# Gate and up by seven half-size products, then the down product by quarters

## The chip, the cores and the metric

One core of a Trainium2 chip runs the kernel. The metric is device time in microseconds (us), the median of three executions. A fourth execution was profiled; all rows below are from it.

## The reference

Two transformer-like blocks over 512 tokens of width 2048, float32, one after the other. Only the last part of the second block changes:

```python
h = rmsnorm_2(x, g_pre_ffn) * (1.0 + sc_f) + sh_f
f = (jax.nn.silu(h @ w_gate) * (h @ w_up)) @ w_down      # 2048 -> 5632 -> 2048
x = x + gt_f * rmsnorm_2(f, g_post_ffn)
```

## The kernel before

Every large product is done in float32 accuracy from three passes: each operand is split into a rounded high part (`fp32r`) and the low rest, and hi·hi, hi·lo and lo·hi are summed in PSUM. The weights stream through a list of *pieces* made in `make_plan`: a piece is 256 rows (two k tiles of 128) by 512 columns. SyncE (SP) loads it as `raw` (four buffers), ScalarE (ACT) rounds it to `whi`, VectorE (DVE) subtracts to get `wlo` (three buffers each); `piece()` keeps the split three pieces ahead of TensorE (PE).

`gemm` consumes pieces: for each k tile and each of four PSUM tiles (banks) it issues the three matmuls. With `half` it does 256 tokens instead of 512. TensorE's order is the order of the program. The other engines are ordered by the tile framework, and each runs its own list strictly in turn. Small work that is to run beside the matmuls (`side`) is issued a step per k tile (`tick`).

The feed-forward part works on `F`, 16 tiles of the transposed activations (they appear as `M` in rows), 128 features by 512 tokens, each in two parts. A *column group* is 256 columns of gate and the same 256 of up, so 22 groups make the 5632 columns. Groups 0 and 1 are done in two token halves, behind the end of the attention output (`w_out2`); the others are one `gemm` of 512 tokens. `up` takes the four PSUM tiles of a group, multiplies silu(gate) by up, and splits the result `u` into two parts that stay in SBUF. After every two groups `down` multiplies those four `u` tiles (stationary, 128 tokens each) by 512 rows of `w_down` and adds the result to `f`. The last `down` is ordered by token blocks, so that the norm, the scaling and the store of one block lie beside the matmuls of the next. PSUM has eight banks: five in the pool `mm`, three in `aux`.

Of the kernel before, what the change touches and what calls it, by code (L numbers as in the profile page):

```python
# [39 lines left out]
class Kernel:  # L40
    def __init__(self, ctx, tc, a, out):
        self.tc, self.nc, self.a, self.out = tc, tc.nc, a, out
        pool = lambda name, **kw: ctx.enter_context(tc.tile_pool(name=name, **kw))
        self.cp = pool("cp", bufs=1)
        self.wp = pool("wp", bufs=1)
        self.t4p = pool("t4p", bufs=30)
        self.t2p = pool("t2p", bufs=8)
        self.bigp = pool("bigp", bufs=1)
# [4 lines left out]
        self.sides = []  # L53
        self.make_plan()


    def make_plan(self):
# [3 lines left out]
        add = lambda segs, k0=0, nk=KT: groups.append((segs, k0, nk))  # L61
# [37 lines left out]
        self.pieces = [(segs, k0 + k) for segs, k0, nk in groups for k in range(0, nk, self.KP)]  # L99
# [3 lines left out]
    FFN = [("u", 0), ("u", 1)] * 2  # L103
    for _n in range(11):
        FFN += [("u", 2 * _n + 2), ("d", _n), ("u", 2 * _n + 3)] if _n < 10 else [("d", _n)]
# [49 lines left out]

    def mm(self):
        return self.mmp.tile([P, S], F32, tag="mm", name=self.name("mm"))
# [4 lines left out]
    def row(self, s):  # L162
        return self.cp.tile([P, S], F32, tag="row", name=self.name(s))
# [25 lines left out]
    def prefetch(self, nload, nsplit):  # L189
        nc, KP = self.nc, self.KP  # L190
        while self.loaded < min(nload, len(self.pieces)):
            segs, k0 = self.pieces[self.loaded]
            raw = self.wp.tile([P, KP, S], F32, tag="raw", bufs=4, name=self.name("raw"))
            o = 0
# [5 lines left out]
            self.raw[self.loaded] = raw  # L200
            self.loaded += 1
        while self.halved < min(nsplit, len(self.pieces)):
            raw = self.raw.pop(self.halved)
            if self.halved < len(self.pieces) - 8:
                hi = self.wp.tile([P, KP, S], F32R, tag="whi", bufs=3, name=self.name("whi"))
                lo = self.wp.tile([P, KP, S], F32R, tag="wlo", bufs=3, name=self.name("wlo"))
            else:
                hi, lo = self.pair("whi"), self.pair("wlo")
            for k in self.parts(self.halved):
                h, l, r = hi[:, k], lo[:, k], raw[:, k]  # L210
                if self.halved < 2 * KT // KP:
# [5 lines left out]
            self.wts[self.halved] = (hi, lo)  # L217
            self.halved += 1
# [131 lines left out]
    def scale_x(self, k):  # L350

        raw, g = self.xt[k], self.cols["norm_gain"][:, k:k + 1]
        pr = self.X[k] = self.pair("X")
        self.act(pr[:, 0, :], raw, AF.Identity, scale=g)
        self.stt(pr[:, 1, :], raw, g, pr[:, 0, :].bitcast(F32), MUL, SUB)
        if k == 0:
            self.ssx = self.const("rxrow", [P, S])
        self.sumsq(self.ssx, raw, k == 0)
# [11 lines left out]
    def ssm_scalars(self):  # L370
# [18 lines left out]
        pr, pi = c("acc1", [P, 9, G]), c("acc2", [P, 9, G])  # L389
# [361 lines left out]
    def ple(self):  # L751
# [6 lines left out]
        acc = [self.const("acc1", [P, S]), self.const("acc2", [P, S])]  # L758
        self.rrow, self.rxrow = self.row("rrow"), self.const("rxrow", [P, S])
# [92 lines left out]
    def ada_steps(self):  # L852
# [4 lines left out]
        def load(i):  # L857
            if i < 192 and i not in st:
                c, kp = divmod(i, 8)
                st[i] = self.t4("wa", [P, 2, S])  # L860
                nc.sync.dma_start(st[i], w[kp * 256:(kp + 1) * 256, c * S:(c + 1) * S].rearrange("(a p) n -> p a n", p=P))

        def step(c, kp):
            load(c * 8 + kp)
            load(c * 8 + kp + 1)
# [299 lines left out]
    def w_out2(self):  # L1165

        nc, a = self.nc, self.a
        mo = []
        acc = [self.const("acc1", [P, S]), self.const("acc2", [P, S])]
        prow, frow = self.row("rrow"), self.const("rxrow", [P, S])  # L1170
# [56 lines left out]
        us = {}  # L1227
        for n in range(2):
            us[n] = self.up(self.gemm(F, half=0), slice(0, 256))
        self.finish(s)  # L1230
        for n in range(2):
            self.up(self.gemm(F, half=1), slice(256, S), us[n])
        self.F, self.M = F, None
# [10 lines left out]
        self.side([lambda b=b, q=q: turn(b, q) for q in range(4) for b in range(4)], 16)  # L1244
        return us

    def up(self, ps, cs=slice(0, S), us=None):

        us = us or [self.pair("u") for _ in range(2)]
        for i in range(2):  # L1250
            t = self.t2("u")
            self.act(t[:, cs], ps[i][:, cs], AF.Silu)
            self.tt(t[:, cs], t[:, cs], ps[2 + i][:, cs], MUL)
            self.nc.scalar.copy(us[i][:, 0, cs], t[:, cs])
            self.tt(us[i][:, 1, cs], t[:, cs], us[i][:, 0, cs].bitcast(F32), SUB)
        return us

    def ffn(self, us):
        nc = self.nc
        f, r, x2 = [], [None] * 4, {}  # L1260
        fv = lambda b, q: f[b * 2 + q // 2][:, q % 2, :]
        out = self.out.rearrange("o s d -> (o s) d")

        def down(n, us):
            if n == 0:
                f.extend(self.t4("f", [P, 2, S]) for _ in range(8))
            for q in range(4):
                ps = self.gemm(us, tok=True)
                for b in range(4):
                    if n == 0:  # L1270
                        nc.vector.tensor_copy(fv(b, q), ps[b])
                    else:
                        self.tt(fv(b, q), fv(b, q), ps[b], ADD)

        def gain():
            co = self.const("cogf", [P, 16])
            self.tt(co, self.mod[:, 80:96], self.cols["g_post_ffn_2"], MUL)
            self.G = self.bigp.tile([P, 4, S], F32, tag="big", name="G")
            for q in range(4):
                self.rows(self.G[:, q, :], co[:, 4 * q:4 * q + 4], 4)  # L1280
                yield

        def x2_load(b, q):
            x2[b, q] = self.t2("x2")
            nc.sync.dma_start(x2[b, q], self.x2d[b * P:(b + 1) * P, q * S:(q + 1) * S])

        ada = self.side([None] * 20 + self.ada(20, 24), 200)
        for kind, n in self.FFN[4:-1]:
            if kind == "u":
                us[n] = self.up(self.gemm(self.F))  # L1290
            else:
                down(n, us.pop(2 * n) + us.pop(2 * n + 1))
            if n == 12 and kind == "u":
                self.finish(ada)
                self.side(self.steps(gain(), 5), 10)
        self.F = None
        us = us.pop(20) + us.pop(21)
        w = [[self.piece() for _ in range(2)] for _ in range(4)]
        ss = self.const("ssf", [P, 4, 4])
        for b in range(4):  # L1300
            for q in range(4):
                x2_load(b, q)
                ps = self.mm()
                for k in range(4):
                    hi, lo = w[q][k // 2]
                    for j, (xi, wt) in enumerate(((0, hi), (1, hi), (0, lo))):
                        nc.tensor.matmul(ps, us[k][:, xi, b * P:(b + 1) * P], wt[:, k % 2, :],  # L1307
                                         start=(k == 0 and j == 0), stop=(k == 3 and j == 2))
                self.tt(fv(b, q), fv(b, q), ps, ADD)
                junk = self.t4("fq", [P, S])  # L1310
                self.act(junk, fv(b, q), AF.Square, accum_out=ss[:, b, q:q + 1])
                self.tt(fv(b, q), fv(b, q), self.G[:, q, :], MUL)
# [3 lines left out]
            for q in range(4):  # L1316
                self.stt(x2[b, q], fv(b, q), r, x2[b, q], MUL, ADD)
                nc.sync.dma_start(out[b * P:(b + 1) * P, q * S:(q + 1) * S], x2[b, q])
# [57 lines left out]
def blocks(K, a, dbg):  # L1376
# [52 lines left out]
    K.ffn(K.w_out2())  # L1429
# [15 lines left out]
```

## Time and profile before

| | us |
|---|---|
| median of 3 executions (3309.81 to 3311.39) | 3310.8 |
| profiled execution, device time | 3309.45 |
| its span, first to last instruction | 3307.4 |
| TensorE busy | 3223.1 (97%) |
| VectorE busy | 1951.2 (59%) |
| ScalarE busy | 1143.7 (35%) |

The device time has 2.05 us more than the span, for what lies around it. Busy time of TensorE counts overlapping matmuls once; a matmul's own record is longer than the step from one matmul to the next, so the step is read from start times.

### The profile page before, as it was taken

The numbers are of one execution on the slowest core, as the hardware profiler recorded it, in microseconds if no ns is written. First come the engines' busy times: TensorE is split into PE (matmuls) and PEld (weight loads), VectorE is DVE, ScalarE is ACT, GpSimd is POOL, SyncE is SP. The second block draws the span as 40 slices with busy tenths as digits, with TensorE's granted clock in tenths as the row PEclk, the third lists the DMA queues.
The fourth block names the chain that finished last, engine by engine and source line by source line (L and its number), as shares of the span: only waits on it lengthen the run. The fifth ranks groups of instructions, "written<-read, shape, count | busy, mean of one in ns | idle before, by whom it ended". The sixth has DMA issues, their size and how long they took to land.

```text
span 3307.4 us, 42034 instructions
## 1 busy us (share of the span) xinstructions
PE 3223.1 (97%) x16076; PEld 2699.6 (82%) x16076; DVE 1951.2 (59%) x3736; ACT 1143.7 (35%) x1679; POOL 15.5 (0%) x28
## 2 busy tenths in 40 slices
PE   7998999999999999999998899999999999999998
PEld 6886887788899777787788888888888888888886
DVE  8569557867798576867748837523333233233336
ACT  6332443223456363434435531222222222222222
POOL 0000000000000000000000000000000000000000
PEclk9999999999999999999999999999999999999999
DMA  6554544756558443434335557433333333333334
GB/s 194 180 194 161 169 156 156 260 168 205 185 172 268 134 141 126 161 128 153 102 106 179 178 173 244 140 97 101 96 96 96 96 96 98 99 96 96 96 98 144
DMA packets 333130, 482.51 MB, mean 146 GB/s; under 512 B 29456, under 2 KB 173968, under 8 KB 332928
## 3 DMA queue, kind: packets, MB, share of 16 engines
q1 hardware_dynamic: 326912, 466.28, 44.3%
q0 software_dynamic: 1664, 5.57, 0.7%
q10 hardware_dynamic: 4352, 7.96, 0.7%
q8 instruction: 126, 2.06, 0.3%
q14 instruction: 76, 0.62, 0.1%
HBM read 454.64 MB, written 25.10 MB: 145 GB/s over the span
## 4 chain that ended last, share of the span: by engine, by line
PE 85%; DVE 10%; DMA 2%; ACT 2%; issue 1%; SPq 0%; DVEq 0%; ACTq 0%
PE mm L245 61%; PE mm L243 18%; DVE wlo L170 2%; PE probs L1009 2%; PE mix L1057 1%; DMA wa<-in_w_ada_dram 1%; DVE sc L170 1%; DVE ada L179 1%; PE turn L1049 1%; ACT whi L215 1%; DVE acc L170 1%; PE mm L595 1%; PE mm L1307 0%; PE mm L596 0%; PE kk L504 0%
## 5 line engine op out<-in xcount | busy, mean ns | idle before, releaser
L170 DVE TENSOR_TENSOR wlo<-raw,whi 128x1024 fp32r<-128x1024 f32 (+1 forms) x607 | 752.9, 1242 | 956.9 <-ACT whi L215 944.5
L215 ACT CAST whi<-raw 128x1024 fp32r<-128x1024 f32 (+1 forms) x607 | 651.1, 1074 | 1591.1 <-PE mm L245 1052.0
L245 PE MATMUL mm<-M,whi 128*128 128x512 f32 (+1 forms) x3840 | 1060.8, 363 | 2.6 <-ACT qk L979 1.3
L245 PEld LDWEIGHTS mm<-M,whi 128*128 128x128 f32 x3840 | 689.8, 190 | 112.4 <-ACT qk L979 1.7
L245 PE MATMUL mm<-M,wlo 128*128 128x512 f32 (+1 forms) x1920 | 695.7, 362 | 5.7 <-DVE wlo L170 5.7
L245 PE MATMUL mm<-H,whi 128*128 128x512 f32 (+1 forms) x2048 | 513.2, 343 | 2.3 <-ACT pp L805 2.3
L245 PEld LDWEIGHTS mm<-M,wlo 128*128 128x128 f32 x1920 | 364.4, 190 | 61.7 <-DVE wlo L170 6.5
L243 PE MATMUL mm<-whi,u 128*128 128x512 f32 x1280 | 395.2, 390 | 1.0 <-ACT u L182 0.8
L245 PEld LDWEIGHTS mm<-H,whi 128*128 128x128 f32 x2048 | 347.1, 191 | 49.2 <-issue 9.8
L245 PE MATMUL mm<-H,wlo 128*128 128x512 f32 (+1 forms) x1024 | 345.9, 338 | 1.5 <-DVE wlo L170 1.5
L245 PE MATMUL mm<-X,whi 128*128 128x512 f32 x1024 | 325.3, 399 | 7.6 <-ACT whi L215 7.2
L179 DVE SCALAR_TENSOR_TENSOR ada<-wa,siluc,ada 128x512 f32<-128x512 f32 x360 | 269.8, 749 | 50.5 <-DMA wa<-in_w_ada_dram 45.3
L243 PEld LDWEIGHTS mm<-whi,u 128*128 128x128 f32 x1280 | 239.7, 188 | 51.6 <-ACT u L182 1.2
L243 PE MATMUL mm<-wlo,u 128*128 128x512 f32 x640 | 249.3, 389 | 0.0
L245 PEld LDWEIGHTS mm<-X,whi 128*128 128x128 f32 x1024 | 190.5, 191 | 48.3 <-ACT whi L215 7.2
L245 PEld LDWEIGHTS mm<-H,wlo 128*128 128x128 f32 x1024 | 194.7, 190 | 22.9 <-DVE wlo L170 1.7
L245 PE MATMUL mm<-X,wlo 128*128 128x512 f32 x512 | 201.6, 394 | 1.2 <-DVE wlo L170 1.2
L243 PE MATMUL mm<-whi,H 128*128 128x512 f32 x512 | 162.7, 399 | 0.0
L243 PEld LDWEIGHTS mm<-wlo,u 128*128 128x128 f32 x640 | 120.2, 188 | 25.0
L170 DVE TENSOR_TENSOR f<-f,mm 128x512 f32<-128x512 f32 x160 | 109.1, 688 | 47.2 <-PE mm L243 45.8
L245 PEld LDWEIGHTS mm<-X,wlo 128*128 128x128 f32 x512 | 97.0, 190 | 23.3 <-DVE wlo L170 2.2
L243 PEld LDWEIGHTS mm<-whi,H 128*128 128x128 f32 x512 | 93.7, 188 | 21.3 <-issue 3.1
(323 smaller groups left out, 2930.6 us busy)
## 6 DMA issues: line engine op xcount, KB each, us to landing
wa<-in_w_ada_dram SPq DMA_DIRECT2D x192, 512.0 KB, 5.9
raw<-in_w_in_dram SPq DMA_DIRECT2D x111, 512.0 KB, 3.7
raw<-in_w_gate_dram SPq DMA_DIRECT2D x192, 256.0 KB, 2.8
raw<-in_w_up_dram SPq DMA_DIRECT2D x192, 256.0 KB, 3.1
raw<-in_w_down_dram SPq DMA_DIRECT2D x88, 512.0 KB, 3.8
raw<-in_w_out_dram SPq DMA_DIRECT2D x80, 512.0 KB, 4.4
raw<-in_w_in_dram SPq DMA_DIRECT2D x130, 256.0 KB, 3.0
raw<-in_w_ple_gate_dram SPq DMA_DIRECT2D x48, 512.0 KB, 4.6
```

The lines of the kernel that those rows point to most:

```text
L170: self.nc.vector.tensor_tensor(o, x, y, op=op)
L179: self.nc.vector.scalar_tensor_tensor(o, x, s, y, op0=op0, op1=op1)
L215: nc.scalar.copy(h, r)
L243: nc.tensor.matmul(ps[i], x[k][:, xi, c], wt[:, a, :], **fl)
L245: nc.tensor.matmul(ps[i][:, cs], wt[:, a, c], x[k][:, xi, cs], **fl)
L595: nc.tensor.matmul(out, self.U[j][:, h, g, :], T[:, :, g, :], start=True, stop=False)
L1009: nc.tensor.matmul(ps[:, :n], q[:, i * P:n], k[:, :n], start=True, stop=True)
L1049: nc.tensor.transpose(pt[:, b * P:(b + 1) * P], p[:, b * P:(b + 1) * P], self.ident)
L1057: nc.tensor.matmul(po[:, :P], pT[:, b * P:(b + 1) * P], v(b, h), start=(b == 0), stop=(b == i))
```

## The change

- The plan no longer alternates. Gate and up come first for all 22 groups: groups 0 and 1 in token halves and group 2 whole, as before; groups 3 to 21 by `seven`. The down product follows, by quarters.
- `seven` (Strassen's scheme in the variant with few additions): the 2048 rows are halved (k tiles k and k+8), the tokens are halved (256 each), and the 256 columns of gate, and those of up, are halved into tiles of 128, so that a group is a product of 2x2 blocks. Seven block products replace eight. Each product runs over 8 pieces k, and in each over gate and up (`s`), with three matmuls of 256 tokens. Seven PSUM banks hold the seven products until the group ends.
- The activations' sums are made once (`sums`, eight calls, during groups 0 to 2). The weights' sums are made for each piece (`halve_sums`): four float32 additions of 128x256 on VectorE, one of them in place in `raw`, and two splits, of the four weight blocks (128x1024: `whi`, `wlo`) and of three sums `T` (128x768: `thi`, `tlo`).
- At the end of a group the four blocks of the result are put together from the seven banks (`ev`: one ScalarE copy `c`, seven VectorE operations), then silu and product (`fin`), and `u` goes to DRAM (`us`) by GpSimd's queue. What comes after product 3 is handed to the next group (`rest`, `todo`), a step after each product. In this stage ScalarE and VectorE run in the order of the program.
- A piece of this stage is loaded by six DMAs instead of two.
- Down by quarters: 512 output columns at a time over all 44 row tiles, summed in PSUM, so that `f` is written once. `u` is read back from DRAM and split again for each quarter (the six pieces at a quarter's turn stay). The last four pieces of the last quarter are ordered by token blocks.

```diff
-        for kind, n in self.FFN:
-            if kind == "u":
-                add([(g2, n * 256, 256), (u2, n * 256, 256)])
-            else:
-                for q in range(4):
-                    add([(d2, q * S, S)], 4 * n, 4)
+        for n in (0, 1, 0, 1, *range(2, self.NS)):
+            add([(g2, n * 256, 256), (u2, n * 256, 256)])
+        for n in range(self.NS, self.NU):
+            groups.append((((g2, n * 256), (u2, n * 256)), range(-8, 0)))
+        for q in range(4):
+            groups.append(([(d2, q * S, S)], self.down_order(q)))
...
+    NU, NS, STAY = DFF // 256, 3, 6
...
+        def one():
+            self.tt(t[:, :, 0], b(0), b(1), ADD)
+            self.tt(b(1), b(1), b(2), ADD)
+            nc.scalar.copy(hv, v)
+
+        def two():
+            self.tt(t[:, :, 1], t[:, :, 0], b(2), ADD)
+            self.tt(t[:, :, 2], t[:, :, 1], b(3), ADD)
+            nc.scalar.copy(th, t)
+
+        self.wts[n] = (hv, lv, th, tl)
+        return [one, two, lambda: self.tt(lv, v, hv.bitcast(F32), SUB), lambda: self.tt(tl, t, th.bitcast(F32), SUB)]
...
+    def sums(self, k):
+        nc = self.nc
+        A, B = self.F[k], self.F[k + 8]
+        x, y = self.t2("sa"), self.t2("sb")
+        for t, pr in ((x, A), (y, B)):
+            v = pr.bitcast(F32)
+            self.tt(t, v[:, 0, :], v[:, 1, :], ADD)
+        s, r = self.t2("s12", (P, 2, 256)), self.t2("s34", (P, 2, 256))
+        self.tt(s[:, 0], y[:, 256:], x[:, 256:], SUB)
+        self.tt(s[:, 1], s[:, 0], x[:, :256], ADD)
+        self.tt(r[:, 0], x[:, :256], x[:, 256:], SUB)
+        self.tt(r[:, 1], s[:, 1], y[:, :256], SUB)
...
+        for pr, src in ((s12, s), (s3, r[:, 0]), (s4, r[:, 1])):
+            nc.scalar.copy(pr[:, 0], src)
+            self.tt(pr[:, 1], src, pr[:, 0].bitcast(F32), SUB)
...
+    def seven(self, n, todo, after):
+        nc = self.nc
+        ps = [(self.mm if j < 5 else lambda: self.aux("p7"))().rearrange("p (w t) -> p w t", w=2) for j in range(7)]
+        c, v, w = (self.t2(x, (P, 2, 256)) for x in ("c1", "cv", "cw"))
+        out = [self.t2(f"c{x}", (P, 2, 256)) for x in (11, 22, 12, 21)]
+        ev = {
+            0: lambda: nc.scalar.copy(c, ps[0]),
+            1: lambda: self.tt(v, ps[1], c, SUB),
+            2: lambda: self.tt(out[0], ps[2], c, ADD),
+            3: lambda: self.tt(w, v, ps[3], SUB),
+            4: lambda: (self.tt(out[1], w, ps[4], SUB), self.tt(v, v, ps[4], SUB)),
+            5: lambda: self.tt(out[2], v, ps[5], SUB),
+            6: lambda: self.tt(out[3], ps[6], w, SUB),
+        }
...
+        for k in range(8):
+            W = self.take()
+            steps = self.ahead() + [lambda: None] * 4
+            plan = {0: steps[0], 1: steps[1], 3: steps[2], 5: steps[3]}
+            for j, (part, slot) in enumerate(self.RIGHT):
+                hi, lo = W[2 * part:2 * part + 2]
+                for s in range(2):
+                    for i, (wt, xi) in enumerate(((hi, 0), (hi, 1), (lo, 0))):
+                        nc.tensor.matmul(ps[j][:, s], wt[:, s, slot], self.C[k][j][xi],
+                                         start=(k == 0 and s == 0 and i == 0), stop=(k == 7 and s == 1 and i == 2))
+                if k == 7 and j == 0:
+                    ev[0]()
+                if j in plan:
+                    plan[j]()
+                if k == 7 and 1 <= j <= 3:
+                    ev[j]()
+                if todo and (k > 0 or j > 0):
+                    todo.pop(0)()
...
+            for n in range(NU - tail):
+                fetch(i + 4, i + 2)
+                hi, lo = self.piece()
+                u, k0 = us.pop(i) if i % NU < NU - R or q == 3 else us[i], order[i][1]
+                for a in range(2):
+                    for b in range(4):
+                        for j, (xi, wt) in enumerate(((0, hi), (1, hi), (0, lo))):
+                            nc.tensor.matmul(ps[b], u[a][:, xi, b * P:(b + 1) * P], wt[:, a, :],
+                                             start=(n == a == j == 0), stop=(n == NU - 1 and a == 1 and j == 2))
+                    self.tick()
```

Where TensorE's list held a whole column group before, one k tile stood as follows: one weight tile after the other, two matmuls with its high part and one with its low part, 512 tokens wide (these rows are two of the four PSUM tiles).

```order
L245 MATMUL mm_20075<-M_14135,whi_20012 128x512 x2
L245 MATMUL mm_20075<-M_14135,wlo_20013 128x512
L245 MATMUL mm_20076<-M_14135,whi_20012 128x512 x2
L245 MATMUL mm_20076<-M_14135,wlo_20013 128x512
L245 MATMUL mm_20077<-M_14135,whi_20012 128x512 x2
L245 MATMUL mm_20077<-M_14135,wlo_20013 128x512
```

Now the first piece of a group by `seven` stands there; shown are product 3, on the sum of activations `s_3092`, product 4, on weights summed (`thi`, `tlo`), and the first rows of products 5 and 6, whose banks `p` are in the pool `aux`.

```order
L1390 MATMUL mm_18732<-s_3092_17355,whi_18608 128x256 x2
L1390 MATMUL mm_18732<-s_3092_17355,wlo_18609 128x256
L1390 MATMUL mm_18733<-s_3091_17354,thi_18611 128x256 x2
L1390 MATMUL mm_18733<-s_3091_17354,tlo_18612 128x256
L1390 MATMUL p_3291_18734<-s_3093_17356,whi_18608 128x256 x2
L1390 MATMUL p_3291_18734<-s_3093_17356,wlo_18609 128x256
L1390 MATMUL p_3292_18735<-M_13800,thi_18611 128x256 x2
L1390 MATMUL p_3292_18735<-M_13800,tlo_18612 128x256
```

Each matmul has half the columns and a weight tile of its own, and a bank takes six of them for each piece (gate and up).

On VectorE, the end of a column group was this: among the splits of coming pieces, two products with the PSUM tiles of up, and two splits of `u`.

```order
L170 TENSOR_TENSOR wlo_20300<-raw_20203,whi_20299 128x1024
L170 TENSOR_TENSOR u_20329<-u_20329,mm_20077 128x512
L170 TENSOR_TENSOR u_20334<-u_20334,mm_20078 128x512
L170 TENSOR_TENSOR wlo_20347<-raw_20234,whi_20346 128x1024
L170 TENSOR_TENSOR u_20327<-u_20329,u_20327 128x512
L170 TENSOR_TENSOR u_20328<-u_20334,u_20328 128x512
```

Now VectorE's list from the last piece of a group into the first piece of the next is as follows. `c_3293` is ScalarE's copy of product 0, `c_3296` to `c_3298` are three of the four result blocks; the two rows that read `mm_18733` read product 4.

```order
L182 TENSOR_TENSOR cv_18737<-mm_18730,c_3293_18736 128x512
L182 TENSOR_TENSOR c_3296_18739<-mm_18731,c_3293_18736 128x512
L182 TENSOR_TENSOR wlo_19201<-raw_19007,whi_19200 128x1024
L182 TENSOR_TENSOR cw_18738<-cv_18737,mm_18732 128x512
L182 TENSOR_TENSOR tlo_19204<-T_19202,thi_19203 128x768
L182 TENSOR_TENSOR T_19282<-raw_19069 128x2x128
L182 TENSOR_TENSOR raw_19069<-raw_19069 128x2x128
L182 TENSOR_TENSOR T_19282<-T_19282,raw_19069 128x2x128 x2
L182 TENSOR_TENSOR c_3297_18740<-cw_18738,mm_18733 128x512
L182 TENSOR_TENSOR cv_18737<-cv_18737,mm_18733 128x512
L182 TENSOR_TENSOR c_3298_18741<-cv_18737,p_3291_18734 128x512
L182 TENSOR_TENSOR wlo_19281<-raw_19069,whi_19280 128x1024
```

The two readers of product 4's bank now stand behind the weight sums of a piece that is needed two pieces later.

## Rows read from the trace of the kernel before

**Rows 1.** The page, parts 1 and 2 (40 equal slices of the span).

```profile
PE 3223.1 (97%) x16076; PEld 2699.6 (82%) x16076; DVE 1951.2 (59%) x3736; ACT 1143.7 (35%) x1679; POOL 15.5 (0%) x28
...
DVE  8569557867798576867748837523333233233336
...
PEclk9999999999999999999999999999999999999999
```

**Rows 2.** Busy time in a stretch (us, busy and count per engine, PEclk, DMA, GB/s).

```profile
2100.00:3200.00 1100.00, 1100.00 (x4863) 910.92 (x4862) 389.04 (x420) 250.34 (x270) 0.00 (x0) 1.00 0.32 97
```

**Rows 3.** TensorE in order of time, 512 wide: start us, us, count at the end.

```profile
2100.19 0.62 PE L245 MATMUL mm<-M,whi 128*128 128x512 f32 x2
...
2108.35 0.62 PE L245 MATMUL mm<-M,whi 128*128 128x512 f32 x2
```

**Rows 4.** TensorE in order of time, 256 wide, in another stage.

```profile
950.04 0.40 PE L245 MATMUL mm<-H,whi 128*128 128x256 f32 x2
...
955.44 0.40 PE L245 MATMUL mm<-H,whi 128*128 128x256 f32 x2
```

**Rows 5.** TensorE's weight loads, 930 to 960 us: busy us, mean ns, idle.

```profile
L245 PEld LDWEIGHTS mm<-H,whi 128*128 128x128 f32 x167 | 26.1, 192 | 0.0
```

**Rows 6.** ScalarE in order of time: the ends of two column groups.

```profile
2199.38 1.28 ACT L182 ACTIVATE u<-mm 128x512 f32<-128x512 f32 x2 [2.58 <-PE mm L245]
...
2242.90 1.28 ACT L182 ACTIVATE u<-mm 128x512 f32<-128x512 f32 x2 [2.58 <-PE mm L245]
```

**Rows 7.** VectorE in order of time, in a stretch where it is full.

```profile
1780.55 0.42 DVE L170 TENSOR_TENSOR acc<-acc,sq 128x256 f32<-128x256 f32 x1
1780.88 0.42 DVE L170 TENSOR_TENSOR mo<-mo,xr 128x256 f32<-128x256 f32 x1
...
1781.55 1.23 DVE L170 TENSOR_TENSOR wlo<-raw,whi 128x1024 fp32r<-128x1024 f32 x1
1782.69 0.43 DVE L170 TENSOR_TENSOR acc<-acc,sq 128x256 f32<-128x256 f32 x1
```

**Rows 8.** VectorE's groups by shape: count, busy us, mean ns, idle.

```profile
L170 DVE TENSOR_TENSOR f<-f,mm 128x512 f32<-128x512 f32 x160 | 109.1, 688 | 47.2 <-PE mm L243 45.8 <-PE mm L1307 1.4
...
L170 DVE TENSOR_TENSOR pw<-acc,bb 128x1024 f32<-128x1024 f32 x8 | 9.7, 1213 | 0.0
```

**Rows 9.** ScalarE's groups by shape: count, busy us, mean ns, idle.

```profile
L215 ACT CAST whi<-raw 128x1024 fp32r<-128x1024 f32 x605 | 649.0, 1074 | 1590.4 <-PE mm L245 1052.0 <-PE mm L243 355.8 <-issue 98.8
...
L1001 ACT COPY v<-mm 128x512 f32<-128x512 f32 x16 | 9.3, 588 | 12.4 <-PE mm L243 11.8
```

**Rows 10.** What TensorE waited for, 1862 to 3300 us: total, times, longest.

```profile
PE mm L1307 <- ACT whi L215: 1.3, 1, 1.3
PE mm L1307 <- DVE wlo L170: 0.8, 2, 0.5
PE mm L243 <- ACT u L182: 0.8, 1, 0.8
```

**Rows 11.** DMA issues: KB each, median us from issue to landing.

```profile
raw<-in_w_gate_dram SPq DMA_DIRECT2D x192, 256.0 KB, 2.8
...
T<-kd POOLq DMA_DIRECT2D x8, 512.0 KB, 7.2
```

**Rows 12.** All engines in order of time, from the last matmul on.

```profile
3295.74 0.39 PE L1307 MATMUL mm<-wlo,u 128*128 128x512 f32 x1
...
3296.89 0.63 ACT L182 ACTIVATE fq<-f 128x512 f32<-128x512 f32 x1
...
3298.26 0.15 DVE L1314 TENSOR_REDUCE s<-ssf 128x1 f32<-128x4 f32 x1
3298.44 0.15 DVE L176 TENSOR_SCALAR rsv<-s 128x1 f32<-128x1 f32 x1
3298.63 0.15 DVE L176 TENSOR_SCALAR rsy<-rsv 128x1 int32<-128x1 int32 x1
...
3300.89 2.74 DVE L179 SCALAR_TENSOR_TENSOR x<-f,rsy,x 128x512 f32<-128x512 f32 x4
```

More of the change, by code (lines that the diff above doesn't have):

```diff
@@ L53, in __init__ @@
         self.sides = []
+        self.ctx = ctx
         self.make_plan()
@@ L60, in make_plan @@
         groups = []
-        add = lambda segs, k0=0, nk=KT: groups.append((segs, k0, nk))
+        add = lambda segs, k0=0, nk=KT: groups.append((segs, range(k0, k0 + nk, self.KP)))
         for c0 in (2048, 0, 1024, 3072):
@@ L154, in const, with wide @@
         return self.cp.tile(list(shape), dt, tag=s, name=self.name(s))
+    def wide(self, s, shape=(P, S)):
+        return self.rowp.tile(list(shape), F32, tag=s, name=self.name(s))
     def mm(self):
@@ L1226, in w_out2 @@
         s = self.side(chain(1), 32)
[L1227 removed]
+        self.us = [self.dram(f"us{n}", [256, S]) for n in range(self.NU)]
         for n in range(2):
[L1229 removed]
+            self.up(n, self.gemm(F, half=0), slice(0, 256))
         self.finish(s)
[L1231 to L1233 removed]
+        self.low.close()
         self.x2d = self.dram("x2d", [S, D])
@@ L1242, in turn, with up @@
             nc.sync.dma_start(self.x2d[b * P:(b + 1) * P, q * S:(q + 1) * S], t)
[L1244 to L1249, printed above, removed]
+        s = self.side([lambda b=b, q=q: turn(b, q) for q in range(4) for b in range(4)], 16)
+        self.F, self.M = F, None
+        if self.NS < self.NU:
+            self.sp = self.ctx.enter_context(tc.tile_pool(name="sp", bufs=1, reuse_waits="tile"))
+            self.C = [None] * 8
+            self.side([None] * 8 + [x for k in range(4) for x in (lambda k=k: self.sums(k), *[None] * 5)], 32)
+        for n in range(2):
+            self.up(n, self.gemm(F, half=1), slice(256, S))
+        self.finish(s)
+        for n in range(2, self.NS):
+            hook = None
+            if n == self.NS - 1 < self.NU - 1:
+                hook = lambda k: self.sums(k // 2 + 1) if k in (6, 8, 10, 12) else None
+            self.up(n, self.gemm(F, hook=hook))
+    def up(self, n, ps, cs=slice(0, S)):
         for i in range(2):
@@ L1261, in ffn, with take, ahead, fetch @@
+    def take(self):
+        while self.halved <= self.at:
+            self.prefetch(0, self.halved + 1)
+        self.at += 1
+        return self.wts.pop(self.at - 1)
+    def ahead(self):
+        self.prefetch(self.at + 5, 0)
+        return self.halve_steps() if self.halved < self.at + 2 else []
+    def ffn(self):
+        nc = self.nc
+        f, x2, us = [None] * 8, {}, {}
         fv = lambda b, q: f[b * 2 + q // 2][:, q % 2, :]
         out = self.out.rearrange("o s d -> (o s) d")
[L1264 to L1273, printed above, removed]
+        order = [(q, k // 2) for q in range(4) for k in self.down_order(q)]
+        raws, ready = {}, [0, 0]
+        NU, R = self.NU, self.STAY
+        def fetch(nload, nsplit):
+            while ready[0] < min(nload, len(order)):
+                i = ready[0]
+                if i < NU or i % NU >= R:
+                    u = order[i][1]
+                    raws[i] = [self.t2("ur") for _ in range(2)]
+                    for j in range(2):
+                        self.tc.keep_in_program_order(
+                            nc.sync.dma_start(raws[i][j], self.us[u][j * P:(j + 1) * P, :]))
+                ready[0] += 1
+            while ready[1] < min(nsplit, len(order)):
+                i = ready[1]
+                if i in raws:
+                    us[i] = [self.pair("u") for _ in range(2)]
+                    for pr, src in zip(us[i], raws.pop(i)):
+                        self.split(pr, src)
+                else:
+                    us[i] = us[i // NU * NU - 1 - i % NU]
+                ready[1] += 1
+        if self.NS < NU:
+            with self.tc.manual_schedule(engines={mybir.EngineType.Activation, mybir.EngineType.DVE}):
+                todo = []
+                for n in range(self.NS, NU):
+                    after = {}
+                    if n == NU - 1:
+                        after = {k: [lambda k=k: fetch(k - 4, k - 5)] for k in (5, 6, 7)}
+                    todo = self.seven(n, todo, after)
+                for g in todo:
+                    g()
+        self.F = self.C = None
@@ L1287, in ffn @@
[L1287 to L1293, printed above, removed]
-                self.finish(ada)
[L1295 to L1298, printed above, removed]
@@ L1299, in ffn @@
-        ss = self.const("ssf", [P, 4, 4])
-        for b in range(4):
[L1301 to L1312, printed above, removed]
+        ss = self.const("ssf", [P, 4, 4])
@@ new lines, in ffn @@
+        fetch(i + 4, i + 4)
+        w = [self.piece() for _ in range(4)]
+        u = [us.pop(i + n) for n in range(4)]
+        for b in range(4):
+            for n in range(4):
+                for a in range(2):
+                    for j, (xi, h) in enumerate(((0, 0), (1, 0), (0, 1))):
+                        nc.tensor.matmul(ps[b], u[n][a][:, xi, b * P:(b + 1) * P], w[n][h][:, a, :],
+                                         start=False, stop=(n == 3 and a == 1 and j == 2))
+            junk = self.t2("fq")
+            self.act(junk, ps[b], AF.Square, accum_out=ss[:, b, 3:4])
+            self.tt(fv(b, 3), ps[b], self.G[1][:, 1], MUL)
```

166 lines of the change are left out of this document (120 added, 46 removed).

## Prediction

> **What bounds the kernel now.** The page comes first [rows 1]: TensorE is busy 97% of the span, at the full granted clock in nearly every slice, and from the middle on VectorE's digits fall to 2 and 3. That is the feed-forward part, the only one that changes: all four compute queues are the same, name by name, up to the second half of the attention output, so nothing ahead of about 1830 us can move. The table by stretches shows what it looks like inside [rows 2]: in 1100 us TensorE is busy for all 1100 at clock 1.00, VectorE for 389. The list of waits says that TensorE lost about 4 us to other engines from 1862 us to the end [rows 10]. So this stage costs the number of matmuls times the step from one to the next, and a change that lowers this product lowers the time by as much, until another engine fills up. What matters, then, is the step at both widths, and how much VectorE can take.
>
> **The step.** At 512 columns the two rows shown lie 36 matmuls apart: 8.16 us / 36 = 0.2267 us each [rows 3]. The kernel already has 256-wide products, with a weight load ahead of each matmul as in the changed kernel: the two rows lie 45 apart, 5.40 / 45 = 0.1200 us [rows 4]. Two of them cost 0.2400, not 0.2267. If a step is a fixed part plus columns, the fixed part is 2 x 0.1200 - 0.2267 = 0.0133 us.
>
> **A column group.** Before: 16 k tiles x 4 banks x 3 = 192 matmuls of 512, 192 x 0.2267 = 43.52 us. ScalarE's rows at the ends of two groups lie exactly 43.52 us apart [rows 6]. After: 8 pieces x 7 products x 2 (gate, up) x 3 = 336 matmuls of 256, 336 x 0.1200 = 40.32 us. Seven eighths of the columns alone would be 38.08; the other 2.24 us are the fixed parts of the narrow matmuls. A group gains 3.20 us, and 19 groups **60.8 us**. This is all that the scheme can give, and it is 59% of the 103 us that one would expect from seven products for eight.
>
> **VectorE in a group.** From rows: 0.42 us for 128x256, a step of 0.33 to the next one when nothing is waited for; 1.23 for 128x1024, step 1.14 [rows 7]; 0.69 for 128x512 with one operand in PSUM [rows 8]. For 128x768, no row: between 0.69 and 1.23, by width 0.95. An instruction that waits for the one ahead of it starts 0.04 us after its end (behind the reduction: 3298.44 + 0.15, then 3298.63 [rows 12]). A piece has four sums (4 x 0.42), the 1024 split and the 768 split: 3.86 us against TensorE's 5.04 for it. The end of a group has seven operations of 0.69 and four of 0.42: 6.5 us. Per group 8 x 3.86 + 6.5 = 37.4 us by whole durations, some 34 by steps, under 40.3. The sums read strided blocks (2x128); an operand read in a pattern costs the same as a plain one in the only such row (1.213 for 1024) [rows 8], so I take 0.42. VectorE goes from 35% to about 90% here, and the average hides what counts: whether it is late at one moment.
>
> **The moment.** Between groups there is no slack in PSUM: seven banks are held, product 4 of the next group takes the bank of product 4 of this one, and TensorE waits until VectorE has read it twice. Time from the start of the last piece (TensorE needs 0.72 us a product; a matmul's record ends 0.16 after the next one could start):
> - ScalarE copies product 0 at 0.94 to 1.53 (0.588 [rows 9]), then casts the coming piece until 2.5 (1.07 [rows 9]).
> - VectorE: `cv` when product 1 is done, 1.64 to 2.33; product 2's row 2.35 to 3.04; the 1024 split from 2.95; `cw` from 4.09; the 768 split from 4.69; then the four sums of the next piece, two of them dependent: 5.56, 6.02, 6.35, 6.81; then the two readers of product 4, 7.15 and 7.75, the second ending at 8.44.
> - TensorE wants that bank at 5.04 + 4 x 0.72 = 7.92 and gets it at 8.48: **0.56 us late**, 18 times: 10.1 us.
>
> If each VectorE operation took its whole duration plus 0.04 the second reader would end at 9.23 and the wait would be 1.35 us (24 us in all); if the sums overlapped a little more it would be 0. Behind the wait, VectorE carries about 3 us of lateness into the next group and works it off at 1.2 to 1.5 us a piece; splits are two pieces ahead, so TensorE sees none of it.
>
> **The way into this stage.** `sums` is eight times about 4.6 us of VectorE (2 x 0.69, 4 x 0.42, 0.69, 2 x 0.42), four of them in the token halves, where a piece lasts only 24 x 0.1200 = 2.88 us and needs 1.14 for its split. Counting VectorE's list along the second half of group 1, it is between 0.1 and 0.4 us late for two or three pieces; bounds 0 and 4 us, as much as TensorE's waits are now in the whole stage [rows 10]; I take 1. In group 2 a piece lasts 5.44 us and the list holds at most 5.8 between splits, with three pieces' lead: nothing.
>
> **Down.** 44 x 4 x 4 x 3 = 2112 matmuls of 512 as before: no change on TensorE. It now has a split of `u` with each piece, 1.23 + 2 x 0.69 = 2.6 us of VectorE per 5.44 us; the adds to `f` are gone. Loads double here, but a weight piece and `u` come three pieces (16 us) ahead, and these DMAs land in 3 to 7 us [rows 11]. `u` written by GpSimd's queue takes about 7 us to land [rows 11], and its buffers are wanted again a group later. Six DMAs a piece instead of two: eight in flight at about 3 us each allow 2.7 per us, 1.2 are needed. I price all this at nothing; if a queue should hold it up, some us.
>
> **The end.** After the last matmul the old chain is add, square, scaling, root, four stores; the new one squares from PSUM and leaves out the add, one 0.69 us operation; two 1024-wide operations replace four of together 2.74 [rows 12]. -0.7 us, between -1.5 and +1.
>
> **Sum**, against the profiled execution: 3309.45 - 60.8 + 10.1 + 1.0 - 0.7 = 3259.1. That execution is 1.35 us below the median of the three others, so 3260 for a median.
>
> **A rule against it.** The weight loads' records last 0.192 us, longer than the step of 0.1200 [rows 4, 5], so successive loads must overlap with each other's records and with matmuls. The Trainium skill (TensorE: Matmul & The Clock Gate, LDWEIGHTS and Part 3) says that a load takes its columns at 1.2 GHz, 107 ns for 128, and overlaps running matmuls only when it targets another row group. All loads here are full, so by that rule (an estimate from the page) a 256-wide step would be 107 + 107 = 213 ns, a 512-wide one 320, and a group would lose 10 us. The trace does not agree: 120 and 227 ns.
>
> **Rivals.**
> 1. VectorE becomes the bound of the whole stage. It decides from 43.5 us a group, where the gain is gone. For it: the 2x128 sums have no row of their own. If they cost as much as 512-wide ones (0.69), a group takes 37.4 + 32 x 0.27 = 46.0 us and the time is 3309.5 + 19 x 2.5 = 3357. Against it: operations overlap by 0.09 us in full stretches [rows 7], and the patterned row. Slower, 3 in 100. A milder form, sums at 0.5 to 0.55 us and readers 1 to 2.5 us late, gives 3268 to 3294: 12 in 100.
> 2. The narrow matmul is paced by its weight load. With 0.192 us a step [rows 5] a group takes 64.5 us and the time is about 3710. The 0.1200 us steps with the same loads speak against it: 1 in 100.
> 3. The change gives nothing: the wait between groups reaches 3.2 us, as it would if TensorE had to wait for the last reader of all seven banks (product 6's, about 2.5 us after product 4's). Then 18 x 3.1 = 56 us go back: 3305. Against it: products 5 and 6 have three banks in turn and come 0.7 and 1.4 us later. With other ways to the same result, 5 in 100; with unknown troubles in the queues of down, slower, 3 in 100.
>
> **Chances.** The forecast's case (no wait to 1.35 us, 3247 to 3277) has 76 in 100, the milder lateness 12, no gain 5, slower 7. The case alone spans 3247 to 3277; the range takes in part of the lateness: 3246 to 3286. A measurement of this kernel tells about 0.2% (6.6 us) from no change; faster than 3304: 0.89; within: 0.04; slower: 0.07.
>
> **What would show it.** Right: 256-wide matmuls 0.120 us apart inside a group, clock 1.00, group ends 40.9 us apart; one TensorE wait per group, at product 4's first matmul, released by VectorE; VectorE at 85 to 95% in this stage; the down stage at 0.2267 us a matmul with no waits. Wrong: a wait at every piece on `wlo` or `tlo` (rival 1), a longer step (rival 2), or waits of 3 us (rival 3). The prediction fails above all if VectorE's sums are slower than 0.42 us.

## The result and the profile after

The changed kernel takes 3257.6 us (median of four executions, 3254.0 to 3259.8) against 3310.3 of the kernel before in the same measurement: a ratio of 0.984, with a 95% interval from 0.9827 to 0.9852. The forecast was 3260, in a range from 3246 to 3286. The profiled execution took 3256.41 us, 53.0 less than that of the kernel before.

The page of the changed kernel, parts 1 and 2, beside [rows 1]:

```profile
PE 3166.4 (97%) x18812; PEld 2786.1 (86%) x18812; DVE 2374.9 (73%) x4659; ACT 1336.4 (41%) x2004; POOL 61.8 (2%) x114
...
DVE  8569557877788576776746977888888887864445
...
PEclk9999999999999999999999999999999999999999
```

VectorE's digits are 7 and 8 where they were 2 and 3, and TensorE's share is 97% as before. The bound is the same engine, with 57 us less busy time. The table by stretches tells the parts apart: the token halves from about 1860 us on, group 2, the 19 groups by seven, and the down product.

```profile
1860.17:1938.16 77.99, 75.60 (x619) 74.95 (x617) 58.00 (x97) 45.97 (x73) 2.16 (x4) 0.98 0.68 210
1938.16:1981.71 43.55, 43.55 (x195) 36.05 (x193) 31.86 (x61) 16.13 (x24) 1.07 (x2) 1.00 0.39 112
1981.71:2760.83 779.12, 770.08 (x6385) 766.95 (x6384) 647.29 (x1103) 307.76 (x398) 39.85 (x74) 1.00 0.41 117
2760.83:3243.56 482.73, 482.50 (x2138) 398.08 (x2136) 279.52 (x398) 180.51 (x256) 2.14 (x4) 1.00 0.66 214
```

The third row is the change: 779.12 us for 19 groups, where 19 plain ones take 19 x 43.52 = 826.9. That is 47.8 of the 53.0 us. VectorE has 647 us to do there, 34.1 a group. It reads as 83% of the stage, and yet TensorE waits for it. TensorE's list of waits from 1862 us on, beside [rows 10]:

```profile
PE mm L1390 <- DVE cv L182: 9.0, 18, 0.5
PE mm L303 <- ACT u L194: 1.9, 1, 1.9
PE mm L303 <- DVE u L182: 0.5, 1, 0.5
PE mm L1500 <- DVE u L182: 0.2, 1, 0.2
```

Eighteen waits of 0.5 us, one at each boundary between two groups. All engines in order of time around one boundary (weight loads, DMA and most matmuls left out):

```profile
2099.07 0.40 PE L1390 MATMUL mm<-M,whi 128*128 128x256 f32 x2
...
2099.99 0.59 ACT L1365 COPY c<-mm 128x512 f32<-128x512 f32 x1 [4.34 <-PE mm L1390]
...
2100.77 0.69 DVE L182 TENSOR_TENSOR cv<-mm,c 128x512 f32<-128x512 f32 x1 [2.13 <-PE mm L1390]
2101.43 0.69 DVE L182 TENSOR_TENSOR c<-mm,c 128x512 f32<-128x512 f32 x1
2102.04 1.22 DVE L182 TENSOR_TENSOR wlo<-raw,whi 128x1024 fp32r<-128x1024 f32 x1
2103.17 0.68 DVE L182 TENSOR_TENSOR cw<-cv,mm 128x512 f32<-128x512 f32 x1
2103.77 0.95 DVE L182 TENSOR_TENSOR tlo<-T,thi 128x768 fp32r<-128x768 f32 x1
2104.64 0.42 DVE L182 TENSOR_TENSOR T<-raw 128x256 f32<-128x256 f32 x1
2105.09 0.42 DVE L182 TENSOR_TENSOR raw<-raw 128x256 f32<-128x256 f32 x1
2105.43 0.88 DVE L182 TENSOR_TENSOR T<-T,raw 128x256 f32<-128x256 f32 x2
2106.23 0.68 DVE L182 TENSOR_TENSOR c<-cw,mm 128x512 f32<-128x512 f32 x1
2106.82 0.68 DVE L182 TENSOR_TENSOR cv<-cv,mm 128x512 f32<-128x512 f32 x1
...
2106.87 0.28 PE L1390 MATMUL mm<-s,wlo 128*128 128x256 f32 x1
...
2107.65 0.48 PE L1390 MATMUL mm<-s,thi 128*128 128x256 f32 x2 [0.50 <-DVE cv L182]
```

The last piece of the group starts at 2099.07. The second reader of product 4 (the last VectorE row) ends at 2107.50, 8.43 us later; the count from durations had given 8.44. Ahead of it stand two splits and four weight sums. The price is more than the idle time shown: the step after 2106.87 should be 0.12 us and is 0.78, so TensorE starts 0.66 late. (Idle time is counted from the end of a record, and that lies 0.16 beyond the next possible start.) ScalarE's copies of product 0 mark the groups:

```profile
2017.90 0.59 ACT L1365 COPY c<-mm 128x512 f32<-128x512 f32 x1 [4.78 <-PE mm L1390]
...
2756.71 0.59 ACT L1365 COPY c<-mm 128x512 f32<-128x512 f32 x1 [4.46 <-PE mm L1390]
```

18 groups lie between: 738.81 / 18 = 41.04 us each, 0.72 above 336 x 0.1200.

The time of a whole run has a part that no edit touched. A transposition at the end of the attention output is the last common point. From there to the last matmul:

| kernel | common point | last matmul starts | between | against the changed kernel |
|---|---|---|---|---|
| before | 1861.38 | 3295.74 | 1434.36 | +51.06 |
| changed | 1860.03 | 3243.33 | 1383.30 | |
| readers first | 1860.17 | 3230.27 | 1370.10 | -13.20 |
| sums moved | 1859.55 | 3239.92 | 1380.37 | -2.93 |
| one group by seven | 1864.93 | 3295.77 | 1430.84 | +47.54 |
| one more sum | 1861.11 | 3252.66 | 1391.55 | +8.25 |
| both | 1861.85 | 3229.54 | 1367.69 | -15.61 |

The common point moves by up to 5 us among runs whose work ahead of it is the same, so a few us are compared between the points, not over the whole. Each row is one profiled execution.

### The profile page after: what moved, and what is told of

Same layout as the page of the kernel before. It is cut to its first block, busy times and chain, and to the rows that moved or that the text cites. A ratio compares the mean times of both kernels' runs of the same rounds, so it can differ in the third digit from the quotient of the medians.

```text
span 3254.7 us, 50767 instructions
## 1 busy us (share of the span) xinstructions
PE 3166.4 (97%) x18812; PEld 2786.1 (86%) x18812; DVE 2374.9 (73%) x4659; ACT 1336.4 (41%) x2004; POOL 61.8 (2%) x114
## 4 chain that ended last, share of the span: by engine, by line
PE 60%; issue 26%; DVE 9%; DMA 2%; ACT 1%; POOL 1%; SPq 0%; DVEq 0%; POOLq 0%; ACTq 0%
PE mm L303 35%; PE mm L1500 13%; PE mm L301 5%; DVE wlo L182 2%; PE probs L1070 2%; POOL us L1378 1%; PE mix L1118 1%; DVE sc L182 1%; DMA wa<-in_w_ada_dram 1%; DVE ada L191 1%; PE turn L1110 1%; ACT whi L250 1%; PE mm L653 1%; PE mm L654 0%; DVE acc L182 0%
## 5 line engine op out<-in xcount | busy, mean ns | idle before, releaser
L250 ACT CAST whi<-raw 128x1024 fp32r<-128x1024 f32 (+1 forms) x455 | 491.9, 1082 | 889.4 <-PE mm L303 496.2
L1500 PE MATMUL mm<-whi,u 128*128 128x512 f32 x1344 | 415.2, 390 | 0.2 <-DVE u L182 0.2
L303 PE MATMUL mm<-M,whi 128*128 128x256 f32 (+1 forms) x1408 | 313.1, 319 | 4.4 <-ACT u L194 1.9
L268 ACT CAST whi<-raw 128x1024 fp32r<-128x1024 f32 x152 | 159.6, 1050 | 366.0 <-DMA raw<-in_w_gate_dram 101.8
L303 PEld LDWEIGHTS mm<-M,whi 128*128 128x128 f32 x1408 | 235.3, 195 | 20.8 <-ACT u L194 2.1
L1390 PE MATMUL mm<-s,thi 128*128 128x256 f32 x1216 | 233.3, 284 | 9.0 <-DVE cv L182 9.0
L1390 PE MATMUL mm<-M,whi 128*128 128x256 f32 x1216 | 232.1, 283 | 0.0
L303 PE MATMUL mm<-M,wlo 128*128 128x256 f32 (+1 forms) x704 | 222.4, 316 | 5.0 <-DVE wlo L182 5.0
L1390 PEld LDWEIGHTS mm<-s,thi 128*128 128x128 f32 x1216 | 189.5, 192 | 12.2 <-issue 12.2
L1390 PEld LDWEIGHTS mm<-M,whi 128*128 128x128 f32 x1216 | 189.9, 192 | 0.1
L1390 PE MATMUL mm<-M,wlo 128*128 128x256 f32 x608 | 172.3, 283 | 0.0
```

What stands on the lines that cost most here:

```text
L268: nc.scalar.copy(hv, v)
L303: nc.tensor.matmul(ps[i][:, cs], wt[:, a, c], x[k][:, xi, cs], **fl)
L1390: nc.tensor.matmul(ps[j][:, s], wt[:, s, slot], self.C[k][j][xi], start=(k == 0 and s == 0 and i == 0), stop=(k == 7 and s == 1 and i == 2))
L1500: nc.tensor.matmul(ps[b], u[a][:, xi, b * P:(b + 1) * P], wt[:, a, :], start=(n == a == j == 0), stop=(n == NU - 1 and a == 1 and j == 2))
```

## The experiments

**Readers first.** In the first piece of a group what was handed over comes ahead of the weight sums.

```diff
+                if todo and k == 0:
+                    todo.pop(0)()
                 if j in plan:
                     plan[j]()
                 if k == 7 and 1 <= j <= 3:
                     ev[j]()
-                if todo and (k > 0 or j > 0):
+                if todo and k > 0:
                     todo.pop(0)()
```

> Edit: in the first piece of a group the operations handed over from the group before come ahead of the weight sums, from the first product on. Theory (the 18 waits at product 4 are VectorE's two readers standing behind the weight sums, and each costs TensorE 0.72 us: 0.50 idle, 0.16 by which a matmul's record outlasts its step, some 0.07 to restart): the readers end 1.2 us earlier, the waits vanish, and the profiled time falls by 18 x 0.72 = 13.0 us to about 3243.5. If only the idle time counts: 9.0 us. Rival (the bank of another product, or the weight sums that are now later, are waited for next): the wait moves to another product or to a split and less than 4 us is gained. Rival (VectorE as a whole is the bound): no change, since it has the same work.

Measured: 3243.9 us (3243.4 to 3244.5), and 13.2 less from the common point. VectorE at the same boundary:

```profile
2102.41 0.95 DVE L182 TENSOR_TENSOR tlo<-T,thi 128x768 fp32r<-128x768 f32 x1
2103.27 0.68 DVE L182 TENSOR_TENSOR c<-cw,mm 128x512 f32<-128x512 f32 x1
2103.87 0.68 DVE L182 TENSOR_TENSOR cv<-cv,mm 128x512 f32<-128x512 f32 x1
2104.47 0.42 DVE L182 TENSOR_TENSOR T<-raw 128x256 f32<-128x256 f32 x1
```

The second reader now ends at 2104.55, and TensorE starts product 4 at 2105.63 without a wait. None of the 18 waits is left and none took their place; the list from 1862 us on has only the two on the way in:

```profile
PE mm L303 <- ACT u L194: 1.9, 1, 1.9
PE mm L303 <- DVE u L182: 0.6, 1, 0.6
```

The copies of product 0 are now 40.32 us apart (2017.99 to 2743.75 over 18 groups), which is 336 x 0.1200. The weight sums had no hurry where they stood. The gain is 0.73 a boundary, which settles what a wait costs: the delay and the restart, not the idle time alone.

**Sums moved.** In the token halves no sum of activations lies at the end of a group any more.

```diff
-            self.side([None] * 8 + [x for k in range(4) for x in (lambda k=k: self.sums(k), *[None] * 5)], 32)
+            at = {3: 0, 9: 1, 18: 2, 24: 3}
+            self.side([(lambda k=at[n]: self.sums(k)) if n in at else None for n in range(32)], 32)
```

> Edit: the four sums of activations made in the token halves start 3, 9, 18 and 24 k tiles in, not 8, 14, 20 and 26, so that none lies at the end of a column group. Theory (TensorE's waits of 1.86 and 0.53 us there come from the sums' casts and subtractions ahead of u on ScalarE and VectorE, and the waits bring the clock down for 16 matmuls, 1.5 us): about 3 us are gained, with one wait of about 1 us left, as the order still has a cast of weights and a copy ahead of u. If the clock still falls, 1.5 us. Rival (u would wait for something else there anyway, such as the late weight transfers): under 0.5 us.

Measured: 3253.5 us (3253.0 to 3256.3), 2.9 less from the common point. The changed kernel at that place, in order of time:

```profile
1911.34 0.91 ACT L1349 CAST s<-s 128x256 fp32r<-128x256 f32 x2
...
1912.16 0.57 ACT L1300 COPY xo<-turn 128x512 f32<-128x512 f32 x1
...
1912.64 0.84 ACT L194 ACTIVATE u<-mm 128x256 f32<-128x256 f32 x2
...
1912.94 1.36 DVE L182 TENSOR_TENSOR s<-s,s 128x512 fp32r<-128x512 f32 x3
1913.07 0.50 PE L303 MATMUL mm<-M,whi 128*128 128x256 f32 x2 [1.86 <-ACT u L194]
...
1914.21 0.75 DVE L182 TENSOR_TENSOR u<-u,mm 128x256 f32<-128x256 f32 x2
...
1914.68 0.80 PE L303 MATMUL mm<-M,whi 128*128 128x256 f32 x2 [0.53 <-DVE u L182]
```

`u`, which frees the banks that TensorE wants, stands behind casts of sums on ScalarE, then behind three subtractions of sums on VectorE. After the two waits TensorE ran at half clock: from 1915.06 to 1917.84 a matmul takes 0.213 us. Half clock is the lower of the two granted levels, 1.2 instead of 2.4 GHz. From 1905 to 1930 us the granted clock is 0.93 in the changed kernel (columns as in [rows 2]):

```profile
1905.00:1930.00 25.00, 22.61 (x175) 22.16 (x173) 19.71 (x36) 12.84 (x22) 1.08 (x2) 0.93 0.65 203
```

With the sums moved it is 1.00 over the same stretch, and one wait of 1.0 us is left, as expected:

```profile
1905.00:1930.00 25.00, 24.01 (x201) 23.75 (x200) 17.78 (x28) 13.19 (x20) 1.08 (x2) 1.00 0.71 223
```

**One group by seven.** Groups 3 to 20 are plain.

```diff
-    NU, NS, STAY = DFF // 256, 3, 6
+    NU, NS, STAY = DFF // 256, 21, 6
```

> Edit: column groups 3 to 20 are done plainly, only group 21 by seven products; the plan, the sums and the down product by quarters stay. Theory (a group by seven gives 3.20 us, each boundary between two takes 0.72 back): 18 x 3.20 - 18 x 0.72 = 44.6 us more than the changed kernel, about 3301 in the profile; that leaves some 8 us below the kernel before, 3.2 from the one group and about 5 from the down product, which no longer has the stalls of the kernel before. Rival (the new order of the plan and the down product by quarters bring a large part): the time stays below 3290. Rival (the down product by quarters costs as much as it saves): 3306.

Measured: 3309.5 us (ten executions, 3305.6 to 3313.0; ratio to before 0.9997, 0.9988 to 1.0007), where 3301 was expected. Its profiled execution reached the common point 4.9 us later than the changed kernel. From there it takes 47.5 more, 44.6 expected, and its waits have two rows that the changed kernel has not, at the start of down:

```profile
2833.39 0.50 PE L1500 MATMUL mm<-whi,u 128*128 128x512 f32 x1 [0.53 <-DVE u L182]
...
2841.09 0.50 PE L1500 MATMUL mm<-whi,u 128*128 128x512 f32 x1 [1.96 <-DVE u L182]
```

By start times these two delay TensorE by 2.8 us; without them it is 44.7: the seven products give what the steps say. What the new order gives by itself, with the way in and these waits paid, is small: 3.5 us from the common point, 3.2 of them the one group. As a time this run is no different from the kernel before, so it can't show the few us of the down product.

**One more sum.** The last weight sum is done twice.

```diff
             self.tt(t[:, :, 2], t[:, :, 1], b(3), ADD)
+            self.tt(t[:, :, 2], t[:, :, 1], b(3), ADD)
```

> Edit: the last of the four weight sums is done twice in each piece (0.42 us more of VectorE, 8 times a group; the values stay). Theory (VectorE has room in a group and is late only at the boundary, where one such sum stands ahead of the readers of product 4): each of the 18 waits grows by 0.34 to 0.45 us, 6 to 8 us in all, about 3263. Rival (VectorE is already the bound of the stage): 8 x 0.34 us in each of 19 groups, 52 us, about 3308. Rival (the wait isn't VectorE's): no change.

Measured: 3267.1 us (3264.7 to 3268.7), 8.25 more from the common point. In the list of waits:

```profile
PE mm L1391 <- DVE cv L182: 17.3, 18, 1.0
```

Each wait grew by 0.46 us: the second sum writes what the first wrote, so it starts 0.46 after it, as a dependent one, where I had taken 0.34 to 0.45. In the rest of the group eight more operations cost TensorE nothing. This is lateness at one moment, not an engine that is full.

**Four more sums.** The same line five times.

> Edit: the last of the four weight sums is done five times in each piece (four times 0.335 us more of VectorE, 32 operations a group; the values stay). Theory (VectorE has some 6 us free in a group of 41 us and becomes the bound of the whole stage when that is used up): busy time per group 34.1 + 32 x 0.335 = 44.8 us, longer than the 40.3 of TensorE, so a group takes 44.8 or a little more and the profile 3256.4 + 19 x 3.8 = 3328, with waits on splits (wlo, tlo) and not only at product 4; slower than the kernel before. Rival (the lateness only adds up at the boundary): 18 x 4 x 0.40 = 29 us more, 3285, all of it at product 4.

Measured: 3429.1 us, ratio 1.036 (1.0341 to 1.0379). Slower was right, the size was not: a group takes 50.6 us, not 44.8, and the profile 3429.9, not 3328. The last sum and its four repeats come 0.46 apart, so 32 operations are 14.7 us and not 10.7 (the row below merges six of them: five steps of 0.46 and a last record of 0.42):

```profile
2302.90 2.72 DVE L182 TENSOR_TENSOR T<-T,raw 128x256 f32<-128x256 f32 x6
```

34.1 and 14.7 are 48.8; in each group VectorE also waits 1.6 us for a result of ScalarE (`c`). TensorE's waits stand not on the splits, as I had expected, but again where the readers of banks stand behind sums:

```profile
PE mm L1394 <- DVE cv L182: 120.2, 35, 4.6
PE mm L1394 <- DVE cw L182: 5.5, 10, 0.6
```

In 500 us of this stage VectorE is busy for 467, and TensorE, which now waits longer, is granted a clock of 0.92:

```profile
2100.00:2600.00 500.00, 429.02 (x3294) 423.49 (x3293) 467.35 (x897) 166.76 (x208) 21.54 (x40) 0.92 0.32 94
```

So the case in which VectorE bounds the stage exists: eight more operations a group are felt at the boundary alone, 32 more make the kernel 119 us slower than before.

**The step against the width, three runs.** Pairs of plain groups with part of their columns, and in the third run with weight tiles of 64 columns, in the kernel with one group by seven; what is left out isn't computed. The edit of the third run is shown; the first two have no `h`, and in them only the first matmul of a bank takes all columns:

```diff
-                    nc.tensor.matmul(ps[i][:, cs], wt[:, a, c], x[k][:, xi, cs], **fl)
+                    d = cs if width is None or fl["start"] or fl["stop"] else slice(0, width)
+                    h = P if stat is None or fl["start"] or fl["stop"] else stat
+                    nc.tensor.matmul(ps[i][:h, d], wt[:, a, i * P:i * P + h], x[k][:, xi, d], **fl)
```

> Edit: as the kernel with one group by seven products, but after its first matmul every bank of the plain groups 5 and 6 takes only 384 of the 512 columns, of groups 9 and 10 only 128, of groups 13 and 14 only 64; the other columns are left out. Theory (a step is 0.0133 us plus the columns at one column per full-speed cycle, here (0.2267 - 0.1200) / 256 = 0.417 ns each): 0.173 us at 384 columns, 0.067 at 128, 0.040 at 64. Rival (a step can't be shorter than the weight load ahead of it): 384 as before, but a floor shows at 64 and 128; by the load's record 0.192 us at both, by the rule of the Trainium skill (TensorE: Matmul & The Clock Gate, LDWEIGHTS) 0.107 us or more at both. Each width is read where VectorE and the transfers keep up, inside a k tile.

> Edit: as the run with narrow groups, with other widths: after its first matmul every bank of the plain groups 5 and 6 takes 320 columns, of groups 9 and 10 224, of groups 13 and 14 192; the other columns are left out. Theory (a step is the larger of 0.0133 us plus 0.417 ns a column, and a floor of 0.112 us seen at 128 and 64 columns): 0.147 us at 320, and 0.112 at 224 and at 192. Rival (no floor at these widths, it only shows where matmuls are as short as their loads): 0.107 at 224, 0.093 at 192.

> Edit: as the kernel with one group by seven products, but between its first and last matmul every bank of the plain groups 5 and 6 takes 128 columns with a weight tile of only 64 columns, and of groups 9 and 10 256 columns with such a tile; the other rows and columns are left out. Theory (the floor of 0.112 us at 128 columns is the load of a weight tile of 128 columns): with half the tile the floor is some 0.056 us and the step at 128 columns is 0.067, by columns. Rival (the floor is what the issue of a load and a matmul takes, whatever their size): 0.112 still. At 256 columns: 0.120 if the fixed 0.0133 us has nothing to do with the load, 0.113 if it is a tenth of the load and halves with it.

TensorE in order of time; in each fence two rows of a kind are so many matmuls apart. First run, 128 columns, 36 apart:

```profile
2229.82 0.39 PE L304 MATMUL mm<-M,whi 128*128 128x128 f32 x2
...
2233.84 0.39 PE L304 MATMUL mm<-M,whi 128*128 128x128 f32 x2
```

Second run, 224 columns, 27 apart:

```profile
2229.83 0.39 PE L304 MATMUL mm<-M,whi 128*128 128x224 f32 x2
...
2232.84 0.39 PE L304 MATMUL mm<-M,whi 128*128 128x224 f32 x2
```

Third run, small weight tiles, 128 columns (51 apart) and 256 (27 apart):

```profile
2079.88 0.22 PE L305 MATMUL mm<-M,wlo 128*64 128x128 f32 x1
...
2082.95 0.22 PE L305 MATMUL mm<-M,wlo 128*64 128x128 f32 x1
...
2199.93 0.28 PE L305 MATMUL mm<-M,wlo 128*64 128x256 f32 x1
...
2202.99 0.28 PE L305 MATMUL mm<-M,wlo 128*64 128x256 f32 x1
```

| columns | weight tile | step, us | by the line |
|---|---|---|---|
| 384 | 128 | 0.173 | 0.173 |
| 320 | 128 | 0.147 | 0.147 |
| 256 | 128 | 0.120 | 0.120 |
| 224, 192 | 128 | 0.1115 | 0.107, 0.093 |
| 128, 64 | 128 | 0.112 | 0.067, 0.040 |
| 256 | 64 | 0.1133 | 0.120 |
| 128 | 64 | 0.0602 | 0.067 |

My line fails below about 236 columns: in a stream of narrower matmuls the step stays at 0.111 to 0.112 us, whatever their width. With half the weight tile it falls to 0.060, so the floor goes by the columns of the weight tile and not by the issue of a load and a matmul. That it is the load itself is the likely reading; the half tile also halves the rows that are written, and no run parts the two. The fixed part goes by the weight tile too: 0.0133 us with a full tile, 0.1133 - 0.1067 = 0.0067 with half of one. The load's record is 0.192 us, longer than the floor, so the record is no price. The Trainium skill (TensorE: Matmul & The Clock Gate, LDWEIGHTS) gives 107 ns for a load of 128 columns; as the pace of successive loads the trace agrees within 5 ns. A list item of the Trainium skill's Part 3 on the same page says that a load overlaps running matmuls only in another row group: these steps contradict it. The Trainium skill's text ahead of that item also lets a load run ahead into a background weight buffer; the steps don't contradict that, but no run here shows such a buffer. So the rule that the prediction held against its forecast was one half of what the Trainium skill says there.

**Both.** The first two edits together.

> Edit: both the handed-over operations ahead of the weight sums, and the sums of activations moved away from the ends of groups. Theory (two separate waits): from a common point ahead of the stage the one gave 13.3 us and the other 2.9; together 16.2, so 3240 in the profile and about 3241 as a median. Rival (they share a cause, or VectorE is late at another place once both are gone): 3243 or more.

Measured: 3241.9 us (five executions, 3240.2 to 3242.7), ratio to before 0.9793 (0.978 to 0.9806). From the common point 15.6 less than the changed kernel, 16.2 expected; a wait of 0.7 us on a split of `u` in the down product is the difference. The two waits had separate causes. With no wait between groups, the 60.8 us of the scheme stand.

## Why the prediction was right, point by point

The forecast missed by 2.4 us, and by 2.7 against its own execution. The terms were not all as good as that: the mechanism of the main ones was right, and the closeness of the sum is partly luck.

- **The step and the group** were right: 0.1200 us at 256 columns, 60.8 us in all, and no load-paced 0.192. The reason given, a fixed part plus columns, holds only because 256 columns lie just above the floor.
- **The moment** was right in place, releaser and cause. The readers' end was foretold within 0.01 us. The size was short: 0.56 us late against 0.72 measured. Left out were 0.15 us from VectorE's end to TensorE's start (0.04 was taken) and about 0.07 to restart. 18 x 0.72 = 13.0 us, not 10.1. Moving the readers gave it all back.
- **VectorE in a group**: 34.1 us, as the count by steps had it. Strided sums cost 0.42. Rival 1 was far enough off, but it begins where operations pile up that depend on each other, 0.46 us apart.
- **The way in** failed in its mechanism. I looked for late weight splits and took 1 us; what came was `u` behind the sums' casts on ScalarE, and then the clock. From the rows: 2.1 us and 0.8 for the two waits with their restarts, 16 x 0.093 = 1.5 at half clock, 4.4 in all; the kernel before lost 0.9 to one wait there. Moving the sums took back 2.9. I had asked whether VectorE is late, and not what stands ahead of the operation that frees a bank.
- **Down** was priced at nothing, and its new part is nothing: 482.7 us with 0.2 of waits. But the waits that the old down product had, [rows 10], are gone, and I never credited them. The stage without the groups by seven gained 51.06 - 47.76 = 3.3 us net, in spite of the way in. In the kernel before, the last down product also lost time to the clock, after its waits:

```profile
3256.00:3264.00 8.00, 6.16 (x20) 4.31 (x19) 5.30 (x7) 3.94 (x8) 0.00 (x0) 0.79 0.12 45
```

How the 3.3 us divide was read from start times, not tested by a run of its own. From the common point to the end of group 2 TensorE takes 11.9 us more than its matmuls' steps, 8.7 in the kernel before (transpositions are in both): 3.2 lost. From there to the last matmul, without the groups by seven, it is 4.0 instead of 10.5: 6.5 gained, with 4.9 of the 10.5 in the last down product.

- **The end**: 11.66 us after the last matmul's start became 11.37, -0.3 for -0.7.
- **Ahead of the stage** this execution was 1.35 us earlier at the common point, by chance.

Sum of the spans: -47.8 - 3.3 - 0.3 - 1.35 = -52.7, as 3307.4 - 3254.7. The forecast's terms add up to -50.4. The boundary cost 2.9 us more than forecast, the way in 2.2, and the end gave 0.4 less; the uncredited 6.5 us of the old order and the 1.35 us of chance more than covered them. These errors have nothing to do with each other, so that they nearly cancel is luck.

## What to carry to other kernels

Price a scheme that saves multiplications by the step of its narrow matmul, and ask first whether that step is still above the pace of the weight loads; here 256 columns are, by 8 ns, and matmuls of half the width would have had nearly the same step (0.112 us). An engine at 83% can make the bound wait: count its list from the release of a bank to the next use, and put the operations that free a bank ahead of those that are needed later, which was worth 13 us for two added lines and a changed condition. Credit the waits that a change removes as well as those it adds, and price a wait by the delay of the next start and by the clock after it, not by its idle time.

## What the runs showed of the hardware that was not expected

- Weight loads of 128 columns come at most every 0.112 us, of 64 columns at least as fast as every 0.060, under matmuls that use the same 128 rows. Their records (0.192 and 0.135 us) overlap.
- In the group with 64 columns TensorE's clock fell to half without a wait ahead: it had been busy throughout, with steps of 0.112 us, and from about 2362.5 us on they are 0.213. With 128 and 192 columns at the same step the clock stayed at 1.00.

```profile
2330.00:2400.00 70.00, 70.00 (x347) 65.07 (x345) 20.19 (x19) 17.06 (x18) 2.16 (x4) 0.73 0.38 121
```

- At half clock a 256-wide step is 0.213 us, which is 1.78 times 0.120 and not twice.
